# Convolution module of an encoder step: one pass over the channel blocks instead of two passes over token halves

## The chip, the cores and the metric

The kernel runs on one core of a Trainium2 chip. Its metric is the device time of one execution in microseconds. The engines are TensorE (PE, with PEld for its weight loads), VectorE (DVE), ScalarE (ACT), GpSimd (POOL) and SyncE (SP), whose queue issues nearly all DMAs.

## The reference

One step of a streaming encoder with width 1024: a convolution module, an FFN, shared keys and values, banded attention with 16 heads, and a second FFN. Two groups of tokens go through it: a prompt of 512 tokens of one new stream, and 8 running streams with 16 new tokens each, 640 tokens in all. Arithmetic is float32. The part that matters here is the convolution module:

```
def conv_module(h, hist, g, w_pw1, b_pw1, w_dw, b_dw, ln_g, ln_b, w_pw2, b_pw2):
    a, gate = jnp.split(rms_norm(h, g) @ w_pw1 + b_pw1, 2, axis=-1)
    glu = a * jax.nn.sigmoid(gate)
    full = jnp.concatenate([hist.astype(glu.dtype), glu], axis=1)
    y = lax.conv_general_dilated(
        full, w_dw[:, None, :].astype(full.dtype), window_strides=(1,), padding="VALID",
        dimension_numbers=("NWC", "WIO", "NWC"), feature_group_count=D_MODEL) + b_dw
    y = jax.nn.silu(layer_norm(y, ln_g, ln_b))
    return h + y @ w_pw2 + b_pw2, full[:, -CONV_HIST:]
```

The depthwise convolution has 31 taps over time, each channel for itself. The prompt starts from 30 rows of zeros, each sample stream from 30 cached rows. The last 30 rows of `full` are outputs too (the "heads" below).

## The kernel before, in words

Activations lie with channels on the 128 partitions: 8 channel blocks of 128, tokens along the free axis. The 640 tokens are cut into two halves of 320: half 0 holds the 128 sample tokens and 192 prompt tokens, half 1 the other 320 prompt tokens. Every large matmul is done as three matmuls of float32 parts (`mm3`, L160 to L162): weights are split by `wsplit` into a high part (ACT, `whi`, L140) and a low part (`wlo`, L144, shared between DVE and POOL by quarters given in `PL1`), activations by `xsplit` (L149, L150). Weight blocks of 1 MB (`raw`) are loaded on SP's queue; `raw`, `whi`, `wlo` have two buffers each.

A list of step names, `PLAN`, sets the order in which the steps of the conv module are written out. The framework keeps each engine's stream in an order of its own that it derives from these steps, their priorities and its own estimates; engines then run in order and wait for semaphores. The steps are:

- `a`, `b`: first projection and gate of one channel block for half 0 or half 1 (`pw1`, `glu`). The 1 MB of weights of a block is loaded and split for each half anew (blocks 0 and 1 of half 0 come from the start).
- `gs` holds, for each channel block, 20 segments of 30 + 16 columns: 8 for the sample streams and 12 for the prompt tokens of half 0, whose overlaps are filled by POOL copies (L575 to L578). `gp` holds half 1 of the prompt as one row.
- The depthwise convolution has 16 tiles (half, block). Ten go to TensorE: `l` writes a block's row to a DRAM scratch (`sc`, L637), reads it back four times shifted (`x4`, L640) and builds diagonal weights `w4` on POOL (L629); `p` does 32 matmuls of 32 output channels (L654; the trace counts 64 records) and ACT adds the bias into `y` (L656). Four go to DVE (`d`, 31 operations each, L619 and L622). Two go to ACT and POOL together (`q`: ACT multiplies, L601, POOL adds, L602).
- `s`: the heads are stored (`out_convs`, `out_convp`).
- `n`: LayerNorm over channels and Silu (`conv_ln`). The mean of a column over 1024 channels is a sum over 8 blocks: `colmean` adds the first `cut` blocks elementwise on POOL (L186) and sums over partitions by 128x1 matmuls with a column of ones (L195), three for each set of 320 tokens. `LCUT` is the cut for the mean, `CUT` (8) that for the squares. `spread` (L207) gives a result back to all partitions. The power of -1/2 is taken on POOL (L234).
- `w`: second projection of a half (`pw2`), 192 matmuls.

After the conv module come the first FFN (`ffn`, its matmuls L352, weight splits L309 and L310), keys and values, and attention for head pairs `p` with tiles `kt`, `qt`, `ohi`, `olo` in the pool `ap`, the output projection for both halves, and the second FFN. The FFN begins with the squares of its RMSNorm (ACT, L167). Pools are placed on top of each other's memory once an earlier pool is closed, and a tile in reused memory waits for the last readers of what lay there.

Of the kernel before, what the change touches and what calls it, by code (L numbers as in the profile page):

```python
# [15 lines left out]
P = 128  # L16
# [13 lines left out]
NS = 20  # L30
GSW = NS * SEG + 4
GPW = HIST + 320 + 2
# [11 lines left out]
CUT, LCUT = 8, 7  # L44
PO = {2: 0, 4: 1}
PL1 = ((0, 2, 2, 2, 2, 2, 2, 2), (0, 0, 0, 3, 0, 0, 0, 2))
# [14 lines left out]
LNO = ((4, 5, 2, 7, 1, 6, 3, 0), (1, 2, 3, 0, 4, 5, 7, 6))  # L61
PLAN = ("a0 y a1 a2 a4 x a3 a5 a6 l04 p04 l05 d02 a7 b6 p05 b1 l07 p07 l06 d01 q00 s0 p06 b2 d03 l11 q16 b3 p11 l12 p12 b0 l13 n0 p13 b4 l10 p10 b5 d15 l14 p14 b7 l17 s1 w0 p17 n1 w1")
# [7 lines left out]
def tile_trunk(ctx, tc, xT, vecs, hist, w_pw1, w_pw2, w_in0, w_out0, w_in1, w_out1,  # L70
# [457 lines left out]
    def load_hist(c0, c1):  # L528
        nc.sync.dma_start(gs[:, c0:c1, 0:8, :], hist[:, c0:c1])
# [3 lines left out]

    gsf = cp.tile([P, KT, GSW], F32, name="gs", tag="gs")
    gs = gsf[:, :, 0:NS * SEG].rearrange("p k (s w) -> p k s w", w=SEG)
    nc.gpsimd.memset(gsf[:, :, NS * SEG:], 0.0)
    nc.gpsimd.memset(gs[:, :, 8, 0:HIST], 0.0)
    nc.gpsimd.memset(gs[:, :, 9, 0:14], 0.0)
    gp = cp.tile([P, KT, GPW], F32, name="gp", tag="gp")
    nc.gpsimd.memset(gp[:, :, HIST + NH:], 0.0)  # L540
# [6 lines left out]
    w00 = wsplit(w_pw1[0], 16, P, cuts=4, pool=PL1[0][0])  # L547
# [3 lines left out]
    w01 = wsplit(w_pw1[1], 16, P, cuts=C01, pool=PL1[0][1])  # L551
    nc.scalar.dma_start(dwv, vecs[:, V_N:])

    def glu(c, g, wh, wl):
        n = gr[g][1]
        ps = []
        for ab in range(2):
            pt = mmt()
            mm3(pt[:, :n], [(wh[:, (ab * 8 + k) * P:(ab * 8 + k + 1) * P],
                             wl[:, (ab * 8 + k) * P:(ab * 8 + k + 1) * P]) for k in range(KT)],  # L560
                xk(xs[g], range(KT)))
            ps.append(pt[:, :n])
        with tc.high_priority(offset=HP):
# [4 lines left out]
            nc.scalar.activation(out=a[:, :n], in_=ps[0], func=AF.Identity, scale=0.5,  # L568
                                 bias=hb1[:, c:c + 1])
            if g == 0:  # L570
                nc.vector.scalar_tensor_tensor(
                    out=gs[:, c, :, HIST:SEG], in0=t[:, :n].rearrange("p (s w) -> p s w", w=SB),
                    scalar=1.0, in1=a[:, :n].rearrange("p (s w) -> p s w", w=SB),
                    op0=ALU.add, op1=ALU.mult)
# [4 lines left out]
            else:  # L579
                nc.vector.scalar_tensor_tensor(out=gp[:, c, HIST:HIST + NH], in0=t[:, :n], scalar=1.0,  # L580
                                               in1=a[:, :n], op0=ALU.add, op1=ALU.mult)

    def conv_pool(c, g):
        n = gr[g][1]
        for j in range(W):
            wj = dcol(V_DW + c * W + j)
            yv = y[g][:, c, :]
            if g == 0:
                src = gs[:, c, :, j:j + SB]
                yv = yv.rearrange("p (s w) -> p s w", w=SB)  # L590
            else:
                src = gp[:, c, j:j + n]
            if j == 0:
                nc.scalar.activation(out=yv, in_=src, func=AF.Identity, scale=wj,
                                     bias=col(V_BDW, c))
                continue
            pr = tp.tile([P, 384], F32, tag="cvt", name=nm("cvt"), bufs=2)
            pv = pr[:, :n]
            if g == 0:
                pv = pv.rearrange("p (s w) -> p s w", w=SB)  # L600
            nc.scalar.activation(out=pv, in_=src, func=AF.Identity, scale=wj)  # L601
            nc.gpsimd.tensor_tensor(out=y[g][:, c, :], in0=y[g][:, c, :], in1=pr[:, :n],  # L602
                                    op=ALU.add)

    def conv(cs, g):
        n = gr[g][1]
        sts = [w2t() for _ in range(0, len(cs), 2)]
        sts = [sts[i // 2][:, i % 2 * 512:i % 2 * 512 + n] for i in range(len(cs))]
        for j in range(W):
            for i, c in enumerate(cs):  # L610
                if g == 0:
                    src = gs[:, c, :, j:j + SB]
                    dst = sts[i].rearrange("p (s w) -> p s w", w=SB)
                else:
                    src = gp[:, c, j:j + n]
                    dst = sts[i]
                wj = dcol(V_DW + c * W + j)
                if j == 0:
                    nc.vector.tensor_scalar(out=dst, in0=src, scalar1=wj, scalar2=col(V_BDW, c),  # L619
                                            op0=ALU.mult, op1=ALU.add)  # L620
                else:
                    nc.vector.scalar_tensor_tensor(out=dst, in0=src, scalar=wj, in1=dst,  # L622
                                                   op0=ALU.mult, op1=ALU.add)
        for i, c in enumerate(cs):
            nc.scalar.activation(out=y[g][:, c, :], in_=sts[i], func=AF.Copy)

    def conv_pe_load(c, g):
        w4 = cp.tile([P, 32, 32], F32, tag="w4", name=nm("w4"))
# [4 lines left out]
        full = GSW if g == 0 else GPW  # L633
        wd = full - 4
        src = gsf if g == 0 else gp
        sc = dr.tile([P, GSW], F32, tag="sc", name=nm("sc"))
        nc.sync.dma_start(sc[:, 0:full], src[:, c, :])  # L637
        x4 = cp.tile([P, 4, full], F32, tag=f"x4{g}", name=nm("x4"), bufs=1 + g)
        for s in range(4):
            nc.sync.dma_start(x4[32 * s:32 * s + 32, :, 0:wd],  # L640
                              sc[:, s:s + wd].rearrange("(q p) w -> p q w", q=4))
        return w4, x4

    def conv_pe(c, g, w4, x4):
        n = gr[g][1]
        pt = mmt()
        for tg in range(8):
            for q in range(4):
                if g == 0:
                    mv = x4[:, q, 0:NS * SEG].rearrange("p (s w) -> p s w", w=SEG)  # L650
                    mv = mv[:, :, 4 * tg:4 * tg + SB]
                else:
                    mv = x4[:, q, 4 * tg:4 * tg + n]
                nc.tensor.matmul(pt[32 * q:32 * q + 32, 0:n], w4[:, 4 * tg + q, :], mv,  # L654
                                 start=(tg == 0), stop=(tg == 7))
        nc.scalar.activation(out=y[g][:, c, :], in_=pt[:, :n], func=AF.Identity,  # L656
                             bias=col(V_BDW, c))

    def conv_ln(g):
# [10 lines left out]
        bc, _ = rstd_bc([y[g][:, c, :] for c in order], n)  # L670
# [23 lines left out]
    def pw1(c, g):  # L694
        wh, wl = wsplit(w_pw1[c], 16, P, pool=PL1[g][c])
        if g == 0:
            load_hist(c, c + 1)
        glu(c, g, wh, wl)

    zs, x4s = {}, {}  # L700

    def step(op, arg):
        g, cs = int(arg[:1] or 0), [int(c) for c in arg[1:]]
        if op == "a":
            if g < 2:
                glu(g, 0, *(w00, w01)[g])
            else:
                pw1(g, 0)
        elif op == "b":
            pw1(g, 1)  # L710
# [4 lines left out]
        elif op == "l":  # L715
            x4s[g, cs[0]] = conv_pe_load(cs[0], g)
        elif op == "p":
            conv_pe(cs[0], g, *x4s[g, cs[0]])
        elif op == "q":
            conv_pool(cs[0], g)  # L720
        elif op == "d":
            conv(cs, g)
        elif op == "s":
            if g == 0:
                nc.sync.dma_start(convs_out, gs[:, :, 0:8, :])
            else:
                nc.sync.dma_start(convp_out, gp[:, :, NH:NH + HIST])
        elif op == "n":
            zs[g] = conv_ln(g)
        elif op == "w":  # L730
            pw2(g, zs[g])
# [8 lines left out]
    tps, early = ExitStack(), ExitStack()  # L740
    xp = early.enter_context(tc.tile_pool(name="xp1", bufs=1, reuse_waits="tile"))
# [281 lines left out]
    for p in range(NP):  # L1023
        bias_load(p)
        if p < NP - 1:
            oT[p] = (ap.tile([P, NT], F32R, tag="ohi", name=nm("ohi"), bufs=3),
                     ap.tile([P, NT], F32R, tag="olo", name=nm("olo"), bufs=3))
        else:
            oT[p] = (ap.tile([P, NT], F32, tag="kt", name=nm("ohi"), bufs=2).bitcast(F32R),
                     ap.tile([P, NT], F32, tag="qt", name=nm("olo"), bufs=QB).bitcast(F32R))  # L1030
# [143 lines left out]
```

## Time and profile before

| what | us |
|---|---|
| median of 3 runs | 1602.44 |
| the three runs | 1599.84 to 1602.8 |
| profiled execution, its own time | 1604.5 |
| span of the profiled execution | 1602.6 |
| TensorE busy in it | 1496.1 |
| conv module (first 302.8 us): TensorE busy | 244.5 |

The page gives one profiled execution: busy times of the engines, the span in 40 slices, the DMA queues, the chain of work that ended last, and the costliest groups of instructions. A group's line names the source line, engine and operation, output and inputs, shapes and count, then busy time with the mean in ns, then the idle time before these instructions and what ended it. Matmuls are pipelined: one lasts some 310 ns in the records, but they follow each other every 147 ns. A table by windows gives, for each stretch of time, the busy time of each engine with its number of instructions, the clock granted to TensorE as a share of full speed, the share of DMA engines busy and GB/s.

### The profile page before, as it was taken

How to read it: one execution, taken by the hardware profiler on the slowest of the kernel's cores; microseconds unless marked ns; L12 is line 12 of the kernel's file. 1: busy time of each engine (PE TensorE's matmuls, PEld its weight loads, DVE VectorE, ACT ScalarE, POOL GpSimd, SP SyncE). 2: the span in 40 equal slices, each digit the busy share in tenths (PEclk: the TensorE clock that was granted, in tenths of full speed). 3: DMA queues.
4: the chain of work that ended last, by engine and by line, in shares of the span. 5: the costliest groups of instructions: out<-in, count | busy, mean ns of one | idle time of the engine just before them, and what ended most of it. 6: DMA issues, size and time to landing. Idle time of an engine off the chain costs nothing.

```text
span 1602.6 us, 26840 instructions
## 1 busy us (share of the span) xinstructions
PE 1496.1 (93%) x10932; PEld 1409.7 (88%) x10932; DVE 1004.7 (63%) x1926; ACT 676.3 (42%) x1293; POOL 282.8 (18%) x323
## 2 busy tenths in 40 slices
PE   5967996999999999999899999998699999999997
PEld 5955695899999999999887798977699999999997
DVE  6892473785665575556666657563675676666555
ACT  5554433453244244245554344441443244244243
POOL 6886543200000000005122201110100000000001
PEclk9988997999999999999999999999699999999998
DMA  7695351302313223224354445451202223213211
GB/s 237 188 261 136 121 157 58 132 27 79 105 54 105 80 73 92 73 80 154 121 200 166 141 160 186 139 188 39 79 27 80 79 79 96 87 56 106 79 53 67
DMA packets 58365, 177.86 MB, mean 111 GB/s; under 512 B 10241, under 2 KB 25985, under 8 KB 48513
## 3 DMA queue, kind: packets, MB, share of 16 engines
q1 hardware_dynamic: 57952, 175.83, 34.2%
q8 instruction: 86, 1.41, 0.4%
q10 hardware_dynamic: 288, 0.31, 0.1%
q14 instruction: 39, 0.31, 0.1%
HBM read 163.65 MB, written 12.47 MB: 110 GB/s over the span
## 4 chain that ended last, share of the span: by engine, by line
PE 86%; POOL 3%; DVE 3%; ACT 3%; DMA 2%; issue 2%; SPq 0%; POOLq 0%; DVEq 0%; ACTq 0%
PE mm L352 35%; PE mm L160 14%; PE mm L162 13%; PE mm L161 13%; PE mm L654 2%; PE w L971 1%; POOL y L602 1%; PE am L956 1%; PE am L939 1%; PE am L1002 1%; POOL acc L186 1%; ACT whi L140 1%; PE w L195 1%; DMA x<-sc 1%; PE w L915 1%
## 5 line engine op out<-in xcount | busy, mean ns | idle before, releaser
L352 PE MATMUL mm<-XH,wlo 128*128 128x320 f32 x736 | 229.1, 312 | 0.7 <-DVE wlo L310 0.7
L352 PE MATMUL mm<-XH,whi 128*128 128x320 f32 x736 | 228.1, 311 | 0.0
L352 PE MATMUL mm<-XL,whi 128*128 128x320 f32 x736 | 225.6, 310 | 0.0
L160 PE MATMUL mm<-xh,whi 128*128 128x320 f32 (+2 forms) x640 | 202.0, 317 | 3.8 <-ACT xh L149 3.4
L161 PE MATMUL mm<-xh,wlo 128*128 128x320 f32 (+2 forms) x640 | 200.7, 315 | 0.6 <-DVE wlo L144 0.6
L162 PE MATMUL mm<-xl,whi 128*128 128x320 f32 (+2 forms) x640 | 197.4, 312 | 0.0
L161 PE MATMUL mm<-hid,wlo 128*128 128x320 f32 (+2 forms) x560 | 172.2, 309 | 0.0
L162 PE MATMUL mm<-hid,whi 128*128 128x320 f32 (+2 forms) x560 | 169.5, 309 | 0.0
L160 PE MATMUL mm<-hid,whi 128*128 128x320 f32 (+2 forms) x560 | 168.1, 309 | 0.0
L309 ACT ACTIVATE whi<-raw 128x1536 fp32r<-128x1536 f32 (+2 forms) x90 | 101.1, 1149 | 145.0 <-PE mm L162 111.0
L310 DVE TENSOR_TENSOR wlo<-raw,whi 128x1536 fp32r<-128x1536 f32 (+2 forms) x90 | 119.5, 1351 | 42.9 <-ACT whi L309 42.8
L352 PEld LDWEIGHTS mm<-XH,wlo 128*128 128x128 f32 x736 | 139.2, 189 | 1.4 <-DVE wlo L310 1.4
L352 PEld LDWEIGHTS mm<-XH,whi 128*128 128x128 f32 x736 | 138.9, 189 | 0.0
L352 PEld LDWEIGHTS mm<-XL,whi 128*128 128x128 f32 x736 | 137.9, 188 | 0.0
L160 PEld LDWEIGHTS mm<-xh,whi 128*128 128x128 f32 x640 | 122.0, 191 | 8.5 <-ACT xh L149 4.0
L161 PEld LDWEIGHTS mm<-xh,wlo 128*128 128x128 f32 x640 | 122.4, 191 | 2.1 <-DVE wlo L144 1.1
L162 PEld LDWEIGHTS mm<-xl,whi 128*128 128x128 f32 x640 | 120.8, 190 | 1.6 <-issue 1.4
L352 PE MATMUL mm<-XH,vhi 128*128 128x320 f32 x368 | 115.2, 313 | 2.8 <-ACT XH L436 2.8
L352 PE MATMUL mm<-XL,vhi 128*128 128x320 f32 x368 | 114.9, 313 | 0.8 <-DVE XL L437 0.8
L352 PE MATMUL mm<-XH,vlo 128*128 128x320 f32 x368 | 115.0, 313 | 0.0
L161 PEld LDWEIGHTS mm<-hid,wlo 128*128 128x128 f32 x560 | 105.3, 188 | 0.0
L162 PEld LDWEIGHTS mm<-hid,whi 128*128 128x128 f32 x560 | 104.6, 188 | 0.0
(210 smaller groups left out, 3463.6 us busy)
## 6 DMA issues: line engine op xcount, KB each, us to landing
raw<-in_w_in SPq DMA_DIRECT2D x38, 1024.0 KB
raw<-in_w_pw SPq DMA_DIRECT2D x22, 1024.0 KB
cache<-in_ck SPq DMA_DIRECT2D x32, 512.0 KB
cache<-in_cv SPq DMA_DIRECT2D x32, 512.0 KB
raw<-in_w_out SPq DMA_DIRECT2D x18, 768.0 KB
raw<-in_w_kq SPq DMA_DIRECT2D x8, 1024.0 KB
x<-sc SPq DMA_DIRECT2D x16, 460.0 KB
raw<-in_w_in SPq DMA_DIRECT2D x12, 512.0 KB
```

The costliest lines, as they stand in the source:

```text
L140: nc.scalar.activation(out=hi[:, a:b], in_=raw[:, a:b], func=AF.Copy)
L160: nc.tensor.matmul(ps, wh, xh, start=(i == 0), stop=False)
L161: nc.tensor.matmul(ps, wl, xh, start=False, stop=False)
L162: nc.tensor.matmul(ps, wh, xl, start=False, stop=(i == last))
L186: eng.tensor_tensor(out=acc[:, :n], in0=prev, in1=s(), op=ALU.add)
L195: nc.tensor.matmul(st[:, 512 + t * w + k:513 + t * w + k], s[:, a:a + P], onec, start=True, stop=True)
L309: nc.scalar.activation(out=hi[:, a:b], in_=src, func=AF.Copy)
L310: nc.vector.tensor_tensor(out=lo[:, a:b], in0=src, in1=hi[:, a:b].bitcast(F32), op=ALU.subtract)
L352: nc.tensor.matmul(pt, wt, v[x][:, k, :], start=(first and k == i == 0), stop=(k == 3 and i == 2), skip_group_check=True)
L602: nc.gpsimd.tensor_tensor(out=y[g][:, c, :], in0=y[g][:, c, :], in1=pr[:, :n], op=ALU.add)
L654: nc.tensor.matmul(pt[32 * q:32 * q + 32, 0:n], w4[:, 4 * tg + q, :], mv, start=(tg == 0), stop=(tg == 7))
L915: nc.tensor.matmul(ps, QQ[:, q], KK[:, 0:n], start=True, stop=False)
```

## The change

Weights of the first projection are loaded and split once for each channel block: step `c` does both halves of blocks 2 to 7 one after the other (blocks 0 and 1: `a`, then `b`). `gs` and `gp` become two parts of one buffer `gall`: 8 sample segments (368 columns) and the prompt as one row of 30 + 512. The overlap copies go, and so does the ACT and POOL convolution.

The depthwise convolution of the prompt is on TensorE for all eight blocks: as one tile of 512 columns for blocks 0 to 4 (`p`), as 192 and 320 columns for blocks 5 to 7 (`A`, `B`). The samples' is on DVE for blocks 0 to 5 (`d01 d23 d45`, 31 operations of 128 columns a block), and on TensorE for 6 and 7 (`S`, with its own shifted rows `x4s`, one buffer). A block's scratch row is 912 columns, written once; `w4` has three buffers, `x4p` three. Both head outputs are stored at one place, `s0`, after the last block.

`PL1` gives the low parts of blocks 2 to 7 to POOL alone. In `conv_ln` the mean's cut is 6 instead of 7 and the squares' cut 1 instead of 8: eight sets of 128x1 matmuls instead of POOL's additions. After the conv module, `kt`, `qt`, `ohi` and `olo` move from pool `ap` to a new pool `op_` that is opened before the activations' pool.

```
-PL1 = ((0, 2, 2, 2, 2, 2, 2, 2), (0, 0, 0, 3, 0, 0, 0, 2))
+PL1 = (0, 2, 4, 4, 4, 4, 4, 4)
-CUT, LCUT = 8, 7
+CUT, LCUT = 8, 6
-LNO = ((4, 5, 2, 7, 1, 6, 3, 0), (1, 2, 3, 0, 4, 5, 7, 6))
-PLAN = ("a0 y a1 a2 a4 x a3 a5 a6 l04 p04 l05 d02 a7 b6 p05 b1 l07 p07 l06 d01 q00 s0 p06 b2 d03 l11 q16 b3 p11 l12 p12 b0 l13 n0 p13 b4 l10 p10 b5 d15 l14 p14 b7 l17 s1 w0 p17 n1 w1")
+LNO = ((0, 1, 2, 3, 4, 5, 6, 7), (0, 1, 2, 3, 4, 5, 6, 7))
+PLAN = ("a0 y a1 x b0 b1 l0 d01 c2 l1 p0 c3 l2 p1 d23 c4 l3 p2 c5 l4 p3 d45 c6 l5 p4 c7 l6 A5 S6 l7 A6 S7 A7 s0 n0 B5 B6 B7 w0 n1 w1")
...
+    gall = cp.tile([P, KT, NSC + NPC], F32, name="gall", tag="gall")
+    gs = gall[:, :, 0:NSC].rearrange("p k (s w) -> p k s w", w=SEG)
+    gp = gall[:, :, NSC:]
...
-                nc.gpsimd.tensor_copy(gs[:, c, 9:NS, 14:30], gs[:, c, 8:NS - 1, 30:46])
-                nc.gpsimd.tensor_copy(gs[:, c, 10:NS, 0:14], gs[:, c, 8:NS - 2, 32:46])
-                nc.gpsimd.tensor_copy(gp[:, c, 14:30], gs[:, c, NS - 1, 30:46])
-                nc.gpsimd.tensor_copy(gp[:, c, 0:14], gs[:, c, NS - 2, 32:46])
...
-    def conv_pool(c, g):
...
+    def conv_load(c):
+        w4 = cp.tile([P, 32, 32], F32, tag="w4", name=nm("w4"), bufs=3)
...
+        sc = dr.tile([P, NSC + NPC], F32, tag="sc", name=nm("sc"), bufs=2)
+        nc.sync.dma_start(sc, gall[:, c, :])
+        return w4, sc
+
+    def conv_shift(sc, tag, a, n, bufs):
+        x4 = cp.tile([P, 4, n], F32, tag=tag, name=nm(tag), bufs=bufs)
+        for s in range(4):
+            nc.sync.dma_start(x4[32 * s:32 * s + 32],
+                              sc[:, a + s:a + s + n].rearrange("(q p) w -> p q w", q=4))
+        return x4
...
-        bc, _ = rstd_bc([y[g][:, c, :] for c in order], n)
+        bc, _ = rstd_bc([y[g][:, c, :] for c in order], n, SQ, 1)
...
+        elif op == "c":
+            w = wsplit(w_pw1[c], 16, P, pool=PL1[c])
             load_hist(c, c + 1)
+            glu(c, 0, *w)
+            glu(c, 1, *w)
...
+            x4s[c] = conv_shift(scs[c][1], "x4p", NSC, NPC - 4, 3)
         elif op == "d":
+            conv(cs)
+        elif op == "S":
+            conv_pe(c, scs[c][0], conv_shift(scs[c][1], "x4s", 0, NSC, 1), -1, NB * SB)
+        elif op in "pAB":
+            a, n = {"p": (0, T), "A": (0, NH - NB * SB), "B": (NH - NB * SB, NH)}[op]
+            conv_pe(c, scs[c][0], x4s[c], a, n)
         elif op == "s":
+            nc.sync.dma_start(convs_out, gs)
+            nc.sync.dma_start(convp_out, gp[:, :, T:T + HIST])
...
+    op_ = early.enter_context(tc.tile_pool(name="op", bufs=1, reuse_waits="tile"))
...
-        kt = ap.tile([P, NT], F32, tag="kt", name=nm("kt"), bufs=2)
-        qt = ap.tile([P, NT], F32, tag="qt", name=nm("qt"), bufs=QB)
+        kt = op_.tile([P, NT], F32, tag="kt", name=nm("kt"), bufs=2)
+        qt = op_.tile([P, NT], F32, tag="qt", name=nm("qt"), bufs=QB)
...
+            oT[p] = (op_.tile([P, NT], F32R, tag="ohi", name=nm("ohi"), bufs=3),
+                     op_.tile([P, NT], F32R, tag="olo", name=nm("olo"), bufs=3))
```

More of the change, by code (lines that the diff above doesn't have):

```diff
@@ L545, in tile_trunk @@
     y = [cp.tile([P, KT, NH], F32, name=f"y{g}", tag=f"y{g}") for g in range(2)]
-    w00 = wsplit(w_pw1[0], 16, P, cuts=4, pool=PL1[0][0])
+    w00 = wsplit(w_pw1[0], 16, P, cuts=4, pool=PL1[0])
     with tc.high_priority(offset=2 * HP):
@@ L550, in tile_trunk @@
     load_hist(0, 2)
-    w01 = wsplit(w_pw1[1], 16, P, cuts=C01, pool=PL1[0][1])
+    w01 = wsplit(w_pw1[1], 16, P, cuts=C01, pool=PL1[1])
     nc.scalar.dma_start(dwv, vecs[:, V_N:])
@@ L583, in conv_pool @@
-    def conv_pool(c, g):
[L584 to L608, printed above, removed]
+            o = HIST + g * NH - NB * SB * g
+            nc.vector.scalar_tensor_tensor(out=gp[:, c, o:o + n - ns], in0=t[:, ns:n], scalar=1.0,
+                                           in1=a[:, ns:n], op0=ALU.add, op1=ALU.mult)
+    def conv(cs):
+        n = NB * SB
+        st = w2t()
+        sts = [st[:, i * 512:i * 512 + n] for i in range(len(cs))]
@@ L624, in conv @@
         for i, c in enumerate(cs):
-            nc.scalar.activation(out=y[g][:, c, :], in_=sts[i], func=AF.Copy)
-    def conv_pe_load(c, g):
-        w4 = cp.tile([P, 32, 32], F32, tag="w4", name=nm("w4"))
+            nc.scalar.activation(out=y[0][:, c, 0:n], in_=sts[i], func=AF.Copy)
+    def conv_load(c):
+        w4 = cp.tile([P, 32, 32], F32, tag="w4", name=nm("w4"), bufs=3)
         nc.gpsimd.tensor_tensor(
@@ L692, in pw2, with step @@
                                                in1=hp(g, m), op0=ALU.add, op1=ALU.add)
-    def pw1(c, g):
-        wh, wl = wsplit(w_pw1[c], 16, P, pool=PL1[g][c])
-        if g == 0:
-            load_hist(c, c + 1)
[L698 to L710, printed above, removed]
+    zs, pws, x4s, scs = {}, {0: w00, 1: w01}, {}, {}
+    def step(op, arg):
+        cs = [int(c) for c in arg]
+        c = cs[0] if cs else 0
+        if op == "a":
+            glu(c, 0, *pws[c])
+        elif op == "b":
+            glu(c, 1, *pws[c])
+        elif op == "c":
+            w = wsplit(w_pw1[c], 16, P, pool=PL1[c])
+            load_hist(c, c + 1)
+            glu(c, 0, *w)
+            glu(c, 1, *w)
         elif op == "y":
```

80 lines of the change are left out of this document (26 added, 54 removed).

## The prediction

> **What bounds the kernel now.** I read the page first (busy time and the chain), then the stretches of the conv stage in a table by windows, then what TensorE waited for, then the chain itself at the places where it leaves TensorE.
>
> ```profile
> span 1602.6 us, 26840 instructions
> ...
> PE 1496.1 (93%) x10932; PEld 1409.7 (88%) x10932; DVE 1004.7 (63%) x1926; ACT 676.3 (42%) x1293; POOL 282.8 (18%) x323
> ...
> PE 86%; POOL 3%; DVE 3%; ACT 3%; DMA 2%; issue 2%; SPq 0%; POOLq 0%; DVEq 0%; ACTq 0%
> ```
>
> TensorE is the bound, and some 106 us of the span are all it leaves idle. The conv stage, which the change rewrites, is the first 302.8 us; these are its worst stretches (columns: time, busy of PE, PEld, DVE, ACT, POOL, granted clock, DMA share, GB/s):
>
> ```profile
> 80.00:117.40 37.40, 23.99 (x196) 21.37 (x194) 36.47 (x60) 20.86 (x35) 33.01 (x33) 0.89 0.98 278
> 117.40:124.80 7.40, 7.27 (x64) 2.99 (x64) 7.04 (x12) 0.00 (x0) 2.00 (x2) 0.62 0.44 105
> 124.80:136.70 11.90, 0.00 (x0) 0.03 (x1) 3.59 (x7) 5.88 (x12) 11.22 (x13) 0.71 0.95 207
> 251.00:270.40 19.40, 6.36 (x31) 5.60 (x31) 5.91 (x17) 5.19 (x12) 7.37 (x9) 0.55 0.17 54
> 270.40:302.80 32.40, 32.40 (x219) 32.40 (x219) 20.05 (x31) 20.27 (x35) 12.13 (x8) 0.96 0.35 118
> ```
>
> ```profile
> PE w L195 <- DVE acc L186: 13.5, 1, 13.5
> PE mm L654 <- DMA x<-sc: 13.5, 2, 12.0
> PE mm L654 <- POOL y L602: 12.0, 1, 12.0
> PE w L195 <- POOL acc L186: 10.5, 2, 8.6
> ```
>
> The first wait is the start, which stays. The second is the depthwise step waiting for its shifted rows, the third a buffer behind POOL's depthwise adds, the fourth POOL's sums of the second LayerNorm. After the first three TensorE is also granted a lower clock.
>
> **The change, step by step: the conv stage.** Prices come from these groups and from the chain.
>
> ```profile
> L654 PE MATMUL mm<-x,w 128*32 128x320 f32 x640 | 52.1, 483 | 25.6 <-DMA x<-sc 13.5 <-POOL y L602 12.0 <-POOL w L629 0.2
> L622 DVE SCALAR_TENSOR_TENSOR w<-gs,dwv,w 128x320 f32<-128x320 f32 x90 | 45.2, 547 | 0.7
> L144 POOL TENSOR_TENSOR wlo<-raw,whi 128x1024 fp32r<-128x1024 f32 x15 | 46.4, 3091 | 32.8 <-ACT whi L140 32.8
> L140 ACT ACTIVATE whi<-raw 128x2048 fp32r<-128x2048 f32 x22 | 41.9, 1905 | 21.0 <-PE mm L162 16.2 <-issue 4.8
> L602 POOL TENSOR_TENSOR y<-y,cvt 128x320 f32<-128x320 f32 x60 | 65.7, 1096 | 12.3 <-ACT cvt L601 9.5
> L674 DVE TENSOR_TENSOR y<-y,w 128x320 f32<-128x320 f32 x16 | 6.5, 482 | 4.5 <-PE w L207 4.5
> ```
>
> ```profile
> 117.47 7.31 PE mm L654 x64
> ...
> 205.38 4.44 PE mm L654 x64
> ...
> 235.97 0.15 PE mm L160
> 236.27 0.15 PE mm L162
> 236.41 0.15 PE mm L160
> ...
> 250.64 0.86 POOL acc L186
> 251.54 1.62 PE w L195 x12
> 253.61 1.66 PE w L207 x6
> ...
> 265.59 0.86 POOL rst L234
> 266.50 1.67 PE w L207 x6
> 268.26 0.50 DVE y L674
> 268.78 1.20 ACT n L676 x2
> 269.98 0.37 ACT xh L149
> 270.39 0.63 PE mm L160
> ```
>
> Two L160 stand 0.44 us apart with two other matmuls between: 0.147 us each. A depthwise tile of 320 tokens is 4.44 us at full clock, 7.31 at the clock of 0.62.
>
> The projections stay 1152 matmuls, 16 x 48 + 2 x 192, 169 us either way. What goes from the path: 13.5 + 12.0 of depthwise waits, some 6 of low clock (7.31 for 4.44 in the quoted tile, about as much again spread over the next two), and POOL's adds of squares in the LayerNorms. Off the path go the 60 POOL adds of 65.7 us with their 60 ACT products, POOL's overlap copies and half of the first projection's weight loads and splits (8 x 1 MB, 8 x 1.9 us on ACT). What comes: depthwise on TensorE for 8 prompt rows of 512 (by columns 4.44 x 512/320 = 7.1 each, 56.8) and for two sample tiles of 128 (1.8 each) instead of ten tiles of 320: 60.4 - 44.4 = +16 us of TensorE; and square sums on TensorE, 16 sets of three 128x1 matmuls. A set's price: 1.62 us for the two sets of twelve records, 0.8 each, +13 us, of which a part lies where TensorE waited anyhow.
>
> Since a stage of waits does not add up by engines, I walk it by hand through the new order of instructions, TensorE's own first:
> - To 36.4 as before. The norm of the second half now has no other matmuls to hide it (steps "x b0 b1"): sums 0.8, power 0.9, spread 0.7, scale, split, in all 4.5 to 5: first matmul at 41.4. b0, b1 are 96 matmuls, 14.1, plus 2 behind VectorE, which runs the eight scalings and splits beside them: 57.5.
> - c2's weights split after b0 frees the buffer: ACT 1.9, then all 2048 columns on POOL, not shown before; twice the 3.1 mean of 1024 is 6.2, the undisturbed ones are near 2.4, so 4.8 to 6.2; I take 4.8. TensorE waits 3.6 (nothing to 5). c2 ends 75.3.
> - p0 c3 p1 c4 p2 c5 p3 c6 p4 c7: 5 x 7.1 + 5 x 14.1 = 106 us, to 181.3. VectorE has per channel 31 sample ops of 128 columns; by the 547 ns of 320 columns between 0.22 and 0.55, I take 0.38, 12 us beside 21. POOL has 2.0 + 4.8 to 6.2 beside 21. Both covered; uncovered they would cost what exceeds 21 per channel.
> - A5, S6, A6: 2.8 + 1.8 + 2.8 = 7.4, to 188.7; sums of the mean to 190.3.
> - S7 needs the sample rows of channel 7. On SP's queue they now stand behind the head output (1.47 MB, issued at about 176, when c7's first half is written), the scratch write, the shifted prompt rows (1.1 MB), a weight block (1 MB) and the single buffer that S6 frees. The scratch write can be issued at 183 and ends by 186; 2.9 MB at the 278 GB/s of the quoted stretch is 10.4 us, and issue and landing some 4: 201. TensorE waits 10.7. At the least (all 4.8 MB streaming from 176) the rows are there at 193.4, a wait of 3; the 12.0 of the quoted wait is the other side. I take 10.7, since the scratch write and read follow each other. S7 and A7, 4.6, then run at low clock, +2.9 by the quoted pair of tiles: 208.
> - First LayerNorm: mean 6 (last copy, sums, spread), eight subtractions 3.5, then squares and their sums mixed with B5 to B7 (13.3): 231.1; power and spread 2.3; scale, Silu, split 2.4: first projection matmul 235.8. VectorE has the second half's eight subtractions ahead of the first split's low part (8 x 0.48 = 3.9, and the eight products), so the products with it wait to 240.7; 192 matmuls and the ragged start end at 270.9.
> - Second LayerNorm: its squares stand on ACT behind a weight split that waits for TensorE, and its power on POOL behind a weight block; eight sums 6.6, power 0.9, spread 0.7 to 1.7, 0.5 + 1.2 + 0.4 to the first matmul: 280.5, against 270.39. The last projection is the 32.4 of the quoted stretch: 312.9 against 302.8.
>
> So the conv stage costs **+10 us**, between 0 (S7 waits 3, c2 nothing, VectorE's second-half subtractions slip aside) and +18 (POOL's splits at 6.2, sums at the low clock's 1.6 instead of 0.8).
>
> On the clock after a wait: the quoted tile stays at 0.62 through its whole 7.4 us. The Trainium skill, "TensorE: Matmul & The Clock Gate", Part 1 (The HAM clock gate), has the array at half rate after an idle window and back at full after about 3.4 us of busy work; by that alone S7 and A7 would lose an estimated 1.7 us, not 2.9, and the sum would be 1 us lower.
>
> **The step at the second FFN.** The tiles of keys, queries and attention outputs move into a pool of their own. Before, the squares of the second FFN's norm take memory that the last pair's tiles still hold:
>
> ```profile
> 1128.57 2.00 ACT L309 ACTIVATE whi<-raw 128x1024 fp32r<-128x1024 f32 x2 [25.84 <-PE mm L162]
> 1130.48 0.45 ACT L167 ACTIVATE sq<-h 128x320 f32<-128x320 f32 x1
> ```
>
> ```profile
> 1129.12 0.16 PE mm L161
> ...
> 1139.79 4.01 PE w L195 x18
> ...
> 1149.30 3.57 PE mm L352 x12
> ```
>
> ```profile
> 302.80:330.00 27.20, 21.70 (x125) 20.37 (x126) 0.87 0.15 54
> 1129.30:1170.00 40.70, 17.13 (x87) 16.23 (x88) 0.66 0.23 78
> ```
>
> ACT idles 25.84 us before a split that needs the last output projection's buffer, with all squares behind it, and TensorE does its first FFN matmul (L352) 20 us after the last projection. The two rows count L352 alone: at the second FFN 87 matmuls, 12.8 us, in 40.7: 27.9 lost. At the first FFN, where the first half's sums are done beside the stage before: 125, 18.4 us, in 27.2: 8.8 lost. In the changed order fifteen of the sixteen squares, the POOL sums, the column sums and the first half's spread stand among the second-half output matmuls, ahead of that split, as at the first FFN. Gain 27.9 - 8.8 = 19.1, less 24 small records that go into TensorE's time (about 3.2): **-16 us**, between -11 (spread again late by the 4.01 of the row) and -19. From the first FFN's body through attention the order is the same in both, so nothing.
>
> Sum: +10 - 16 = -6. On the profiled execution, 1604.5 (1.9 more than its span), 1598.5; the median of the runs is 2.1 lower, 1602.44, so **1597**.
>
> **Rivals.**
> - The conv stage gets no longer: sums and VectorE's chains fall into TensorE's gaps, S7's rows come at 194. For it: 36 us of quoted waits go, against +16 of depthwise. Against: the LayerNorm chains lie at the end, with nothing beside them. 1602.4 - 16 - 2 = 1584 to 1588.
> - Slower: the shifted rows come late at each prompt step. Every p waits for a write to memory and a read back, on one queue that also holds weight loads waiting for POOL's split of two channels earlier. For it: the 12.0 us wait for the same rows before. Against: two channels of lead, 40 us. At 3 us for each of p0 to p4, +15: 1612. It decides from 2 us each (9 us in all turn -6 into a loss over 0.2%).
> - The pool does nothing: the squares find another tile to wait for, or TensorE takes the same 20 us for another reason. Then only +10 is left: 1612.
> - By a rule of order on the DMA side, S7's rows wait only for bytes, not for issue: 4.8 MB at 278 GB/s from 176 gives 193.4, the gap shrinks to 3 and the time is 1590, inside my forecast's range. The Trainium skill, "DMA: Bandwidth & Descriptors", section Queues, rings and completion order, says that each engine takes descriptors in ring order; it does not undo the write that the read must follow, so I weigh it at the low end.
>
> **Chances.** Forecast (1590 to 1604, its own range) 0.45; no longer conv stage 0.20; late rows 0.24; pool without effect 0.11. A difference under 0.2%, 3.2 us, could not be told from none. Faster: 0.32 of the forecast and 0.20 of the first rival, 0.52; same: 0.11 and 0.04 of the late rows, 0.15; slower: 0.02, 0.20 and 0.11, 0.33. The range 1584 to 1612 leaves out the outer halves of the first and last rivals and some tail, about 0.2.
>
> **What the profile after would show.** First FFN matmul at about 313 if the conv stage is right, and within 5 us of the last output projection if the pool step is. TensorE waits for shifted rows once, about 10 us near 190; p0 to p4 follow their projections without a wait; the second projection's first half starts near 236, its second near 280. The forecast is wrong if waits of several us stand before p1 to p4, if TensorE is idle over 5 us at the second FFN, or if depthwise on 512 columns is not 7.1 us.

## The result and the profile after

The changed kernel takes 1610.68 us (median of 6 runs, 1607.68 to 1615.77), the kernel before beside it 1601.19 (1598.41 to 1604.35): a ratio of 1.0059, 95% interval 1.0039 to 1.0080. It is slower by 9.5 us, where 6 us less was forecast. The time lies in the stated range (1584 to 1612), but on the other side of the kernel before.

The profiled execution of the changed kernel took 1610.26 us with a span of 1608.3. Its page (busy times and the chain):

```profile
span 1608.3 us, 27216 instructions
...
PE 1521.2 (95%) x11220; PEld 1426.8 (89%) x11220; DVE 967.9 (60%) x1984; ACT 635.4 (40%) x1233; POOL 193.4 (12%) x209
...
PE 89%; DVE 4%; DMA 3%; issue 2%; ACT 1%; POOL 1%; POOLq 0%; DVEq 0%; ACTq 0%; SPq 0%
```

POOL, ACT and DVE lost 167 us of busy time together; TensorE gained 25. Every line number is one lower up to the step functions (L159 to L161 are the projections, L351 the FFN, L622 the depthwise matmuls). What TensorE waited for in the first 345 us of the kernel after (total, times, longest):

```profile
PE w L194 <- DVE acc L185: 17.0, 1, 17.0
PE mm L622 <- DMA x4s<-sc: 12.1, 1, 12.1
PE w L206 <- POOL rst L233: 6.6, 3, 3.2
PE mm L159 <- ACT xh L148: 5.6, 4, 2.2
PE mm L160 <- POOL wlo L143: 2.5, 1, 2.5
```

The two waits of 12 us in the middle of the stage are gone. One of 12.1 has come, near its end, and the one at the start has grown from 13.5 to 17.0. The stretches of the stage (time, busy of PE, PEld, DVE, ACT, POOL, clock, DMA share, GB/s) show where it sits:

```profile
77.90:184.40 106.50, 106.50 (x804) 80.38 (x808) 36.12 (x101) 24.45 (x40) 34.73 (x14) 1.00 0.53 146
184.40:193.00 8.60, 8.40 (x204) 7.06 (x196) 1.72 (x2) 3.52 (x5) 4.96 (x3) 1.00 0.59 105
193.00:205.00 12.00, 0.07 (x4) 0.10 (x8) 0.00 (x0) 0.00 (x0) 2.71 (x4) 0.52 0.88 218
205.00:217.70 12.70, 12.70 (x201) 8.88 (x202) 0.34 (x2) 0.81 (x3) 0.00 (x0) 0.78 0.01 3
217.70:241.00 23.30, 22.34 (x212) 16.00 (x208) 5.96 (x18) 8.00 (x16) 1.72 (x2) 0.86 0.00 1
241.00:280.00 39.00, 37.74 (x234) 37.66 (x234) 16.55 (x32) 17.27 (x26) 10.62 (x4) 0.87 0.24 79
280.00:318.00 38.00, 32.29 (x206) 31.83 (x207) 25.80 (x37) 21.11 (x37) 14.23 (x10) 0.87 0.31 101
```

From 77.9 to 184.4 TensorE has no gap at all and the full clock. All the new loss lies before and behind that, and from 193 on the clock is under 0.9 in every row. These shares are means over phases: cut in pieces of 1 us, the clock is 0.50 from 194 to 210, 1.00 to 234, 0.50 to 251, 1.00 to 282 and 0.50 to 292. The first FFN matmul (L352 before, L351 after):

```profile
306.42 0.42 PE L352 MATMUL mm<-XH,vhi 128*128 128x320 f32 x1 [0.32 <-ACT XH L436]
```

```profile
325.12 0.42 PE L351 MATMUL mm<-XH,vhi 128*128 128x320 f32 x1 [0.32 <-ACT XH L435]
```

So in these two executions the conv stage is 18.7 us longer. Other executions with the same conv stage, of runs told below, put this matmul at 322.79 (changed) and at 303.01 and 307.61 (before), so a difference of a few us between two traces at this point can be chance. The first matmul of the second FFN is only 7.3 us late (1156.63 against the 1149.30 shown before), the span 5.7: something is won back at the second FFN, as forecast. The difference of the spans is smaller than that of the medians because the profiled execution of the kernel before, at 1604.5, was one of its slower ones.

### The profile page after: what moved, and what is told of

It reads as the page before. It is cut to its first block, busy times and chain, and to the rows that moved or that the text cites. A ratio compares the mean times of both kernels' runs of the same rounds, so it can differ in the third digit from the quotient of the medians.

```text
span 1608.3 us, 27216 instructions
## 1 busy us (share of the span) xinstructions
PE 1521.2 (95%) x11220; PEld 1426.8 (89%) x11220; DVE 967.9 (60%) x1984; ACT 635.4 (40%) x1233; POOL 193.4 (12%) x209
## 4 chain that ended last, share of the span: by engine, by line
PE 89%; DVE 4%; DMA 3%; issue 2%; ACT 1%; POOL 1%; POOLq 0%; DVEq 0%; ACTq 0%; SPq 0%
PE mm L351 34%; PE mm L159 15%; PE mm L161 14%; PE mm L160 14%; PE mm L622 3%; DMA cache<-in_ck 1%; PE w L941 1%; PE am L926 1%; PE am L972 1%; PE am L909 1%; PE w L885 1%; DMA x4s<-sc 1%; PE w L886 1%; PE w L206 1%; PE w L194 1%
## 5 line engine op out<-in xcount | busy, mean ns | idle before, releaser
L351 PE MATMUL mm<-XH,wlo 128*128 128x320 f32 x736 | 229.1, 312 | 1.6 <-DVE wlo L309 1.6
L351 PE MATMUL mm<-XH,whi 128*128 128x320 f32 x736 | 227.3, 311 | 0.0
L351 PE MATMUL mm<-XL,whi 128*128 128x320 f32 x736 | 225.6, 309 | 0.0
L159 PE MATMUL mm<-xh,whi 128*128 128x320 f32 (+2 forms) x640 | 204.2, 321 | 6.2 <-ACT xh L148 5.6
L161 PE MATMUL mm<-xl,whi 128*128 128x320 f32 (+2 forms) x640 | 197.7, 316 | 0.0
L161 PE MATMUL mm<-hid,whi 128*128 128x320 f32 (+2 forms) x560 | 169.4, 308 | 0.0
L159 PE MATMUL mm<-hid,whi 128*128 128x320 f32 (+2 forms) x560 | 167.7, 308 | 0.0
L351 PEld LDWEIGHTS mm<-XH,wlo 128*128 128x128 f32 x736 | 139.2, 189 | 2.9 <-DVE wlo L309 2.9
L351 PEld LDWEIGHTS mm<-XH,whi 128*128 128x128 f32 x736 | 138.6, 189 | 0.0
L351 PEld LDWEIGHTS mm<-XL,whi 128*128 128x128 f32 x736 | 138.3, 189 | 0.0
L159 PEld LDWEIGHTS mm<-xh,whi 128*128 128x128 f32 x640 | 124.5, 195 | 12.3 <-ACT xh L148 6.6
L161 PEld LDWEIGHTS mm<-xl,whi 128*128 128x128 f32 x640 | 122.2, 193 | 1.6 <-issue 1.4
L351 PE MATMUL mm<-XH,vhi 128*128 128x320 f32 x368 | 115.0, 313 | 0.3 <-ACT XH L435 0.3
L351 PE MATMUL mm<-XL,vhi 128*128 128x320 f32 x368 | 114.5, 312 | 0.9 <-DVE XL L436 0.8
L351 PE MATMUL mm<-XH,vlo 128*128 128x320 f32 x368 | 114.8, 312 | 0.0
L161 PEld LDWEIGHTS mm<-hid,whi 128*128 128x128 f32 x560 | 104.6, 188 | 0.0
```

The source lines that it names most:

```text
L159: nc.tensor.matmul(ps, wh, xh, start=(i == 0), stop=False)
L161: nc.tensor.matmul(ps, wh, xl, start=False, stop=(i == last))
L351: nc.tensor.matmul(pt, wt, v[x][:, k, :], start=(first and k == i == 0), stop=(k == 3 and i == 2), skip_group_check=True)
```

## The experiments

**The two halves of the change, apart.** The first run is the kernel before with the pool alone, the second the changed kernel without it.

```diff
+    op_ = early.enter_context(tc.tile_pool(name="op", bufs=1, reuse_waits="tile"))
...
-        kt = ap.tile([P, NT], F32, tag="kt", name=nm("kt"), bufs=2)
+        kt = op_.tile([P, NT], F32, tag="kt", name=nm("kt"), bufs=2)
```

> The kernel before with one part of the change alone: keys, queries and attention outputs in a pool of their own, opened before the activations' pool. Theory A (the pool alone lets the squares of the second FFN stand ahead of the weight split): the first FFN matmul comes about 5 us after the last output projection instead of 20, the conv stage ends where it did, and the time falls by 13 to 17 us, to about 1586. Theory B (the gain at the second FFN comes from the new order of the whole program, not from the pool): under 3 us.

> The changed kernel with keys, queries and attention outputs back in the attention pool. Theory A: 13 to 17 us slower than the changed kernel, about 1625, with the 20 us gap back at the second FFN. Theory B: within 3 us of the changed kernel, 1611.

The pool alone gives 1593.49 us, ratio 0.9946 (0.9931 to 0.9961), 9.1 under the 1602.63 of the kernel before beside it. The changed kernel without the pool takes 1620.21, 9.5 over the changed kernel. The pool is worth about the same in both, so theory A holds in kind, and its size of 13 to 17 does not. The conv stage's part of the change alone costs 1620.21 - 1602.63 = 17.6 us.

**The start.** The diagonal weights (`w4`) are made to wait for the second half's norm.

```diff
+            i4z = cst.tile([P, 32], F32, name="i4z", tag="i4z")
+            nc.gpsimd.tensor_scalar(out=i4z, in0=xs[1][1][:, 0, 0:32].bitcast(F32), scalar1=0.0,
+                                    scalar2=None, op0=ALU.mult)
+            nc.gpsimd.tensor_tensor(out=i4, in0=i4, in1=i4z, op=ALU.add)
```

> The changed kernel with the diagonal weights built only after the second half's norm: the small diagonal gets a sum with zero times a column of that norm's low part, so the three builds can't stand at the start. Theory A (POOL's three builds slow VectorE's squares and sums at the start, 2.08 us for 0.49): the first column sum starts at 13.5 us or a little earlier instead of 17.0, and the conv stage ends 3.5 to 5 us earlier, 1606. Theory B (the input's arrival sets the start, the builds only lie beside it): still about 17, no change. A third way: the builds then stand between the norm and the third block's split on POOL and cost back what they gave at the start.

The timeline of the changed kernel at the start, and of this run:

```profile
6.06 6.30 POOL L598 TENSOR_TENSOR w<-i,dwv 128x1024 f32<-128x1024 f32 x3 [3.49 <-DMA dwv<-in_vecs]
...
6.40 2.08 DVE L169 TENSOR_TENSOR sq<-h 128x320 f32<-128x320 f32 x1
8.40 4.90 DVE L185 TENSOR_TENSOR acc<-acc,sq 128x320 f32<-128x320 f32 x3
```

```profile
6.34 0.49 DVE L169 TENSOR_TENSOR sq<-h 128x320 f32<-128x320 f32 x1
6.85 1.02 DVE L185 TENSOR_TENSOR acc<-acc,sq 128x320 f32<-128x320 f32 x2
```

Beside POOL's builds a VectorE operation of 0.49 us takes 2.08. The kernel before has one build there, and the same square beside it takes 2.08 too:

```profile
5.90 2.08 POOL L629 TENSOR_TENSOR w<-i,dwv 128x1024 f32<-128x1024 f32 x1 [3.21 <-DMA dwv<-in_vecs]
...
6.25 2.08 DVE L170 TENSOR_TENSOR sq<-h 128x320 f32<-128x320 f32 x1
```

Without the builds the first column sum starts at 12.4 us instead of 17.0, and the first FFN matmul comes 4.8 us earlier, at 320.31. The input's arrival at 5.2 us is not what sets it: theory A. The median, 1609.08, is 1.6 us lower; the rest lies in the spread of the runs (1607.59 to 1610.62), so the gain is shown by the stage, not by the total.

**The wait for the last sample rows, by its queue.** Heads go out channel by channel, and `x4s` has two buffers.

```diff
+            nc.sync.dma_start(convs_out[:, c], gs[:, c])
...
-            nc.sync.dma_start(convs_out, gs)
...
-            conv_pe(c, scs[c][0], conv_shift(scs[c][1], "x4s", 0, NSC, 1), -1, NB * SB)
+            conv_pe(c, scs[c][0], conv_shift(scs[c][1], "x4s", 0, NSC, 2), -1, NB * SB)
```

> The changed kernel with the sample heads stored channel by channel after each channel's scratch write, and two buffers for the shifted sample rows. Theory A (the wait before the last sample tile is the queue: 1.47 MB of heads ahead of the rows): the 12.1 us wait falls to 5 to 8, and with less idle the clock after it stays higher, 6 to 9 us earlier in all, about 1603. Theory B (the wait is the way out and back, the write to memory and two reads after the last projection, and the heads only lie beside it): 10 us or more of wait remain, 0 to 2 us.

9.3 of the 12.1 us remain, the first FFN matmul comes at 323.78 (1.3 earlier, less than two traces of one stage differ by), the time is 1610.73. That is theory B, nearly: 2.8 us were the queue or the single buffer, which this run changes together. The chain of the changed kernel shows the rest as one way:

```profile
184.95 0.50 DVE gall L575
185.47 2.78 DMA sc<-gall
188.32 6.74 DMA x4p<-sc
195.08 9.76 DMA x4s<-sc
204.93 7.25 PE mm L622 x128
```

The last gate, the write, the prompt rows and the sample rows: 20 us from the end of the last projection to the tile that starts on them. The fourth row runs from the issue of the last quarter of the sample rows; the first quarter was issued at 191.60. In the wait the DMA engines are 0.88 busy (the row from 193.00 above), so the way is bytes as well as latency. Sending the sample rows ahead of the prompt rows was not tried.

**The wait, filled and removed.** One run puts B5 and B6 ahead of S7. The other takes channel 7's samples off the way through memory (channel 5's go there in their place), gives `x4s` two buffers and moves B5 ahead of A7.

```diff
-... c7 l6 A5 S6 l7 A6 S7 A7 s0 n0 B5 B6 B7 w0 n1 w1
+... c7 l6 A5 S6 l7 A6 B5 B6 S7 A7 s0 n0 B7 w0 n1 w1
```

> The changed kernel with two of the three deferred prompt tiles (B5, B6) moved ahead of the last sample tile (S7); everything else, the late rows of S7 with them, as in the changed kernel. Theory A (what the wait costs is TensorE's idle time and the low clock after it, for B5 and B6 are not needed where they stood, in a LayerNorm that TensorE fills with them): the 12.1 us wait falls to about 3, the clock after it stays at 1.0, and the first FFN matmul comes 8 to 12 us earlier. Theory B (the path is the way of channel 7's sample rows through memory to the LayerNorm, and filling it buys nothing: A7 still ends near 212, and the LayerNorm then has too little beside its chain): under 3 us, and only having channel 7's samples elsewhere, as in the run with VectorE, gives the 16 us.

```diff
-... p3 d45 c6 l5 p4 c7 l6 A5 S6 l7 A6 S7 A7 s0 n0 B5 B6 B7 w0 n1 w1
+... p3 d4 c6 l5 p4 c7 d7 l6 A5 S5 l7 A6 S6 B5 A7 s0 n0 B6 B7 w0 n1 w1
```

> The changed kernel with the samples of the last channel on VectorE and those of channel 5 on TensorE instead, two buffers for the shifted sample rows, and one deferred prompt tile (B5) moved ahead of A7. Theory A (the 12 us before the last sample tile are one exposed way through memory): TensorE no longer waits for sample rows, has B5's 4.4 us while A7's rows come, and the first matmul of the second projection comes 6 to 11 us earlier: about 1602. Theory B (the wait moves on to A7's rows or to VectorE's 31 operations): under 3 us.

Filled, S7 still starts when its rows are there:

```profile
205.98 3.64 PE L622 MATMUL mm<-x4s,w 128*32 128x128 f32 x64 [5.88 <-DMA x4s<-sc]
```

TensorE's wait is halved, yet the first matmul of the second projection comes at 240.77 against 241.14, and the time is 1609.94 (1607.80 to 1615.16), the changed kernel's. The first FFN matmul comes at 321.61, 3.5 us earlier in this one trace. Removed, in the chain of that run:

```profile
184.84 13.18 PE mm L622 x320
198.04 0.54 ACT y L628
198.58 0.27 issue
198.85 2.81 PE mm L622 x64
201.66 1.65 PE w L194 x14
```

TensorE goes through; A7 ends at 201.7 instead of 212.2, the first FFN matmul comes at 309.13, 16.0 earlier, and the time is 1597.06, 13.6 less than the changed kernel's, ratio 0.9967 (0.9955 to 0.9980). What the run changes undoes the larger part of the stage's loss. The way through memory is not all of it: the second projection's first matmul comes 7.5 us earlier (233.68), that of its second half 15.0. Between the two, the chains of the changed kernel and of this run differ on POOL:

```profile
277.73 1.92 ACT whi L139
279.72 3.38 POOL wlo L143
283.21 0.85 POOL rst L233
...
287.92 0.64 PE mm L159
```

```profile
259.84 1.92 ACT whi L139
261.83 3.44 POOL wlo L143
...
268.31 0.86 POOL rst L233
...
272.91 0.64 PE mm L159
```

In the changed kernel the power of the second LayerNorm (`rst`) stands behind POOL's part of the fourth weight split, in this run behind the third and ahead of the fourth. By these chains about half of the 16 us is the way through memory, and the other half the place of one POOL operation in an order that the framework derives; which of the run's edits moved it was not tried. As to the way itself, the path costs more than TensorE's idle time: filling half of the wait with other work moved the second projection's start by 0.4 us. VectorE had room for the 31 operations (36 of 106.5 us busy in the stretch to 184.4, 1.7 in the next).

**Where the squares are added.**

```diff
-        bc, _ = rstd_bc([y[g][:, c, :] for c in order], n, SQ, 1)
+        bc, _ = rstd_bc([y[g][:, c, :] for c in order], n)
```

> The changed kernel with the squares' cut of the LayerNorms back at 8 (POOL adds the squares, one set of column sums instead of eight). Theory A (TensorE is full in the first LayerNorm: 22.3 of 23.3 us busy from 217.7 to 241.0, while POOL is busy 1.7 us): the first matmul of the second projection comes 3 to 6 us earlier than 241.1, and the second half's, at 287.9, moves with it: 3 to 6 us faster. Theory B (POOL's chain of adds, 0.94 us each, is as long as what it replaces, and in the second half it stands behind weight blocks): within 2 us, or up to 5 slower.

Both hold, one after the other. The second projection's first matmul comes at 234.50, 6.6 us earlier, as theory A says. Then the second half waits for POOL's chain,

```profile
PE w L194 <- POOL acc L185: 11.7, 1, 11.7
```

and the first FFN matmul is only 2.3 us earlier (322.87), the time 1611.21, the same. Together with late weights, heads by channel and the last channel on VectorE:

> The changed kernel with the late diagonal weights, heads by channel, the last channel on VectorE and the squares' cut of 8, all at once. If the parts add up as stages: start -4.8, last sample tile -6 to -11, squares -3 to -6, so 12 to 20 us faster than the changed kernel, 1591 to 1599. If the ends of the LayerNorm chains hold whatever comes before them, only the start is left: 1606.

1597.73 us, and the first FFN matmul at 312.36: no better than the last channel alone. The parts do not add, since POOL's 11.7 us in the second LayerNorm stand there again. Without that edit and without the heads by channel they do:

> The changed kernel with the two parts that gained: the last channel's samples on VectorE, and the diagonal weights built after the second half's norm. If the stages add up: first FFN matmul 4.5 to 5 us earlier than with the first part alone (309.1), at 304 to 305, and 1592 to 1594 in time. If the start's gain is lost again at the third block's split, 309 and 1597.

The first FFN matmul comes at 304.46, and the time is 1593.06, ratio 0.9928 (0.9903 to 0.9953).

**What the pool gives and what is given back.** In the kernel after, ACT's timeline before the last output projection is

```profile
1118.32 1.06 ACT L308 ACTIVATE vhi<-raw 128x1024 fp32r<-128x1024 f32 x1
1119.91 1.06 ACT L308 ACTIVATE vhi<-raw 128x1024 fp32r<-128x1024 f32 x1 [0.54 <-PE am L926]
1120.99 0.60 ACT L148 ACTIVATE ohi<-am 128x512 fp32r<-128x512 f32 x1
```

and TensorE's there and at the second FFN:

```profile
1121.64 0.42 PE L159 MATMUL mm<-ohi,whi 128*128 128x320 f32 x1 [1.80 <-ACT ohi L148]
...
1151.47 0.31 PE L161 MATMUL mm<-olo,whi 128*128 128x320 f32 x1
...
1156.63 0.61 PE L351 MATMUL mm<-XH,vhi 128*128 128x320 f32 x1
```

Two splits of FFN weights now stand ahead of the last attention output, so the first output matmul waits 1.80 us instead of 0.69. The output projection itself, in the kernel before, in the changed one and in the kernel before with the pool (same columns as the stretches above):

```profile
1102.78:1129.41 26.63, 26.19 (x174) 25.53 (x174) 7.95 (x16) 0.84 (x1) 0.00 (x0) 1.00 0.00 1
```

```profile
1121.64:1151.78 30.14, 28.99 (x198) 28.20 (x198) 11.56 (x24) 7.74 (x16) 5.29 (x6) 1.00 0.11 36
```

```profile
1101.79:1134.55 32.76, 31.73 (x198) 30.80 (x198) 11.55 (x24) 7.73 (x16) 5.25 (x6) 0.90 0.09 33
```

The 24 records more are the sums of the FFN's norm; at full clock they make 3.5 us. In the third row part of the stretch is also at a lower clock. Two runs put the two splits at ordinary priority, behind the attention output.

```diff
-                with tc.high_priority(offset=HP):
+                with tc.high_priority(offset=0 if small and l else HP):
```

> As the run before, with the first two weight splits of the second FFN at ordinary priority, so that on ACT they stand behind the split of the last attention output and not ahead of it. Theory A (those two splits make the first output matmul wait 1.8 us for 0.7, and that idle time lowers the clock for the output projection): from the last store of keys to the last output matmul 3 to 6 us less, 1588 to 1590. Theory B (the low clock there comes from the attention's small products and would come anyhow): 1 us or less.

> The kernel before with the pool, the late diagonal weights and those two splits at ordinary priority: the same question in the other kernel. Theory A: 3 to 6 us under 1592. Theory B: 1 us or less. Against the run before it tells which of the two conv stages is the better one when both have what helped: by stages the changed one should be ahead or behind by at most 3 us.

The wait falls to 0.73 and 0.72 us, but the times are 1592.79 (against 1593.06 with the splits ahead) and 1590.27 (1588.48 to 1593.41, against 1591.95 for the run below): within the spread, theory B. The second of them has the conv stage before and the first the repaired one, so with the pool the rewritten stage is not ahead either. The run below is the kernel before with the pool and the late weights, the two splits left where they were:

> The kernel before with the pool and with its first diagonal weights built after the second weight block instead of beside VectorE's squares at the start. The one build beside them made one square last 2.08 us instead of 0.49: the first column sum comes 1 to 2 us earlier, and the time is 1 to 2 us under the pool alone, 1592, or the same if the start is made up for by the later wait for shifted rows.

1591.95 us (1591.16 to 1592.62), ratio 0.9941; the first column sum starts at 12.6 us instead of 13.5.

To see whether the low clock comes with the pool, four kernels without it were profiled:

> The changed kernel with the last channel's samples on VectorE and late diagonal weights, without the pool. Theory A (the low clock in the last attention pair comes with the pool): its stretch from the last store of keys to the output projection is at most 45.5 us and the output projection 26.6 at a clock of 1.00; Theory B (it comes in any execution): 44 to 50 us, and an output projection of 27 to 29.5 at a clock of 0.9 in most. In time: 9 us over the same kernel with the pool, 1602, which would make the repaired conv stage worth nothing against the kernel before.

> The kernel before, unchanged, once more, for its last attention pair. Theory A: 45.5 us or less and 26.6 us at a clock of 1.00. Theory B: 44 to 50 and 27 to 29.5 as likely as not.

> The kernel before with late diagonal weights and no pool, for its last attention pair. Theory A: 45.5 us or less and 26.6 us at a clock of 1.00. Theory B: 44 to 50 and 27 to 29.5 as likely as not.

> The changed kernel with the last channel's samples on VectorE, without the pool, for its last attention pair. Theory A: 45.5 us or less and 26.6 us at a clock of 1.00. Theory B: 44 to 50 and 27 to 29.5 as likely as not.

| last attention pair, us | six executions without the pool | twelve with it |
|---|---|---|
| last key store to output projection | 41.8 to 46.9, mean 44.9 | 44.0 to 49.9, mean 47.0 |
| output projection | 26.6 in each | 30.1 to 32.9, mean 31.8 |
| end of it to the first FFN matmul | 19.7 to 20.1, mean 19.9 | 4.5 to 5.2, mean 5.0 |

The first line varies in both groups, so theory B holds there. The second does not: no execution without the pool is above 26.65, and nine of twelve with it are over a microsecond above the 30.1 that the added records explain. That part of theory A is borne out; what starts the low clock is open, since it came in one of the two runs with the splits out of the way as well (31.65 us; 30.24 in the other). In time, the repaired conv stage without the pool takes 1601.69, ratio 0.9993 (0.9979 to 1.0007): as fast as the stage before. Once repaired, the rewritten conv stage neither gains nor costs; the same kernel with the pool takes 1593.06, so what the best version of it gains comes with the pool.

## Why the prediction was wrong

The sum was +10 for the conv stage and -16 for the second FFN. Measured by the runs with one half each, it is +17.6, and -9.1 or -9.5. The mechanisms were there; both sizes were off the same way.

**Conv stage, step by step** (in the two profiled executions, +18.7):
- *"To 36.4 as before"* failed. The start is 3.5 us later, because three builds of `w4`, not one, stand beside VectorE's squares. The change's three buffers were costed as storage; that they let POOL run three builds at once, at the worst place, was not. The run with late weights shows it. The Trainium skill ("GPSIMD Engine Reference", section 1, Specifications) says that POOL shares its SBUF interfaces with VectorE and contends with VectorE instructions that have two SBUF inputs; the trace agrees, with 2.08 us for 0.49. The row with 2.08 stood in the profile of before, for one build.
- Gap of the second half's norm and b0, b1: from first projection matmul to c2's start 36.8 us instead of 38.1 by the walk. c2's wait for its split was 2.5 us (taken: 3.6), POOL's 2048 columns 4.55 (taken: 4.8). Right or better, but c2's matmuls then took 15.2 us instead of 14.1, with the clock at half from 64 to 67.
- p0 to c7: 106.5 against 106, 7.00 for a prompt tile against 7.1, none late. The rival of late rows was wrong.
- S7: 12.1 against 10.7, and S7 with A7 7.25 against the 7 of the walk. Right, by the way named. (The quoted tile of before did not stay at 0.62 throughout: in pieces of 1 us its clock is 0.50 up to 123 and full behind it, and S7's is 0.50 up to 210.) But the reasoning priced it as a gap of TensorE. The runs show it as the path: filling half of it moved the second projection by 0.4 us, taking it out brought A7's end 10.5 us forward. Its price was already in the sum (13.6), so this does not explain the miss; it tells where much of the stage's loss lay.
- The two LayerNorms and projections: 29.0 from A7 to the first matmul against 27.8, 46.8 to the second half's against 44.7, and 37.2 to the FFN against 36.0 before. Together 4.4 us, with a granted clock of 0.78 to 0.87 in all stretches from 205 to 318, where the walk had full-clock durations save for S7 and A7. From 241 to 251, in the phase at half clock, the second projection's matmuls follow each other every 0.27 us; in the kernel before they begin at 0.15. Part of the difference is addition: the walk's terms of the second LayerNorm, set end to end behind 270.9, give 281.2 or more, not 280.5.

The step that failed is the sum of small serial terms at full clock: 3.5 at the start, 1.3 more between c2's end and S7, and 4.7 from there on, less 0.9 between the start and c2's end, make the 8.6 between +10.1 and +18.7. The 3.5 is shown by a run. That the low clock made most of the 4.7 is read from the traces and not shown by a run that changes the clock alone, and 4.7 is not far above what two traces of one stage differ by.

**Second FFN.** The gap behind the output projection shrank by 14.9 us, from 19.9 to 5.0, for the reason given, and with the pool alone too. What failed is *"From the first FFN's body through attention the order is the same in both, so nothing"*: the order of the last pair differs by two weight splits, and its output projection became 5.2 us longer on average. 3.5 of that were foreseen as 3.2; the other 1.7, and some 2 before the projection, came with the wait of 1.8 us and the low clock. The gain behind the projection itself was sized well: in the first 40.7 us TensorE does 205 FFN matmuls instead of 87, at 0.147 us 17.3 us of the 19.1 forecast. Less 5.2 and 2.1, 10.0 remain, near the 9.1 and 9.5 measured.

**The rivals.** The pool without effect was wrong, though its 1612 is close to the time measured. No longer conv stage: wrong as the change stands, and right (0.9993) once one channel is moved and the builds are late. S7's rows behind bytes alone, with a wait of 3: wrong, 9.3 remained with the heads out of the way. The chances put 0.33 on slower; what tipped it, three builds beside the start, half-clock phases in the LayerNorms and a longer output projection, was not among the rivals.

## What to carry to other kernels

A transfer out to memory and back is hidden only while there is other work that does not lead to it: when a stage is reordered, look which item now comes last, and give that one the route without the trip. An added buffer lets work start earlier, so price where it will then run and what runs beside it. A gain that removes a wait should be counted up to the next common point, not at the wait: of 14.9 us, 9 arrived.

## What the runs showed of the hardware that was not expected

- Beside a POOL tensor-tensor operation on 128x1024 (2.08 us), a VectorE square of 128x320 took 2.08 us instead of 0.49; beside three of them, three adds took 4.90 instead of 1.60.
- In pieces of 1 us, the granted clock in the first 345 us of these traces is 0.50 or 1.00 but for the pieces in which it changes; other shares are means over both. In the changed kernel it fell to 0.50 at 234 although TensorE was recorded busy without a gap for the 5 us before, in 128x1 column sums and depthwise matmuls, and it came back at 251, after 10 us of nearly gapless work in the second projection.
- One output projection of 198 recorded matmuls took 30.1 to 32.9 us in different executions, with a mean granted clock of 1.00 to 0.90. In the traces of the changed kernel (30.14) and of the run with all parts in (32.86) the 198 stand in the same order; in the second the clock is 0.50 for some 6 us soon after the start.
- The last quarter of the 0.75 MB of shifted sample rows landed 9.8 us after its issue with a weight block queued ahead of the sample rows, and 8.8 us after it with the block queued behind them.
